# Two-layer hybrid trunk: SGU constants in another buffer, a planner that reckons a longer landing, and the last tile's sums kept in PSUM

## The chip, the cores and the metric

The kernel runs on one core of a Trainium2 chip. The metric is the device time of one execution in microseconds (us). Before the change the median of three runs is 1430.35 us (1429.0 to 1435.49).

## The reference, cut to what matters

Two layers run on a latent stream x of 512 tokens and a context of 256 tokens, both 1024 wide. Only the latent stream is returned, so the second layer (layer 1 below) keeps 512 rows at its end.

```
shift, scale, gate = split(silu(c) @ w_ada + b_ada, 3)
h = x * (1 + scale) + shift
a_q, ..., s_u, s_v, s_g, m_a, m_g, m_s = split(h @ w_in)
y_attn = attention(q, k_all, v_all) * silu(a_g)
y_gla  = gla_finish(o_forward + o_backward) * silu(g_g)
vn     = layer_norm(s_v, sgu_ln_g, sgu_ln_b)
mixed  = einsum('gts,bnsgc->bntgc', w_s, vn) + b_s
y_sgu  = s_u * mixed * silu(s_g)
m      = sigmoid(m_a) * (y_attn @ w_br_attn) + sigmoid(m_g) * (y_gla @ w_br_gla) + sigmoid(m_s) * (y_sgu @ w_br_sgu)
x_new  = layer_norm(ALPHA * x + gate * (m @ w_out), post_g, post_b)
```

All of it is float32. The kernel splits each float32 operand into a high and a low part and makes three matmuls of every product (high by high, high by low, low by high).

## The kernel before, in words

**A planner writes the order.** The program text does not run in its own order. Every operation goes through `_Eng` or `Sched.alt` into `Sched.record`, and `Sched.order` (from L225) then places all of them by a list simulation: each operation has a cost, dependencies, a priority and the buffers (tags, each with some slots) that it needs. `issue` repeats this 16 times with corrected priorities and emits the shortest plan. The result is one fixed order per engine (PE, DVE, ACT, POOL, and SP, which issues the DMAs). So a changed constant can move instructions anywhere. Two choices are the planner's as well: `tta` (an elementwise operation of two tensors) may go to DVE or POOL, `evac` to ACT or DVE. Since all is recorded through one place, nearly every instruction of the trace carries L421 (or L128 for those with two possible engines, L119 for grouped matmuls).

How the planner times a DMA is in these lines, L325 to L328: the transfer occupies the DMA engines for `cost`, and whoever waits for the data may start 700 ns later.

```
            if e == "SP":
                dma = max(dma, st + 1300.0) + cost
                free[e] = max(st + 60.0, dma - self.AHEAD)
                end = dma + 700.0
```

**The parts of a layer.** Projections of h with the columns of `w_in` (weights stream in as `raw` tiles of 256 KB and are split into `hi` on ACT and `lo` on DVE or POOL), attention, GLA, the SGU, then the branches `brA`, `brG`, `brS` (products of each branch with its weight, gated and summed into `mac`), and last the product with `w_out`, the residual sum and the layer norm. Projections that nothing needs soon are fill work: they are projected when PE would else have nothing to do (matmuls `p<-hlh,hi` and the like), parked in DRAM (the gates `m_a`, the SGU inputs), and loaded again later as `kept` or `sv`.

**The SGU of layer 1** (from L1224). `sv` (the parked s_v) is normalised per tile: bn_stats, bn_aggr, POOL's rsqrt, one `tensor_scalar`, then times `lg` and plus `lb`. `sgc` holds the constants `lg`, `lb`, `bs` and `wsT`, 256 KB each. Each normalised tile is multiplied with `wsT` on PE (matmuls `pt<-sgc,sv`); DVE adds `bs` and writes `ymix`, which is then multiplied with two loaded gates. `sgc` lies in tag "T3". Its only slot holds the attention output `yat` until `ysplit` has split it into `yh` and `yl`; after `sgc` the slot goes to `mac0`.

**The branches** (`branch`, in the same function). Branch A multiplies `yh`, `yl` with `w_br_attn`: matmuls `p<-yh,hi`, `p<-yl,hi`, `p<-yh,lo`, 12 to a group of output channels. The tag "p" has two PSUM slots. A slot is free when DVE has made `mac` from it, which needs the sigmoid of the parked gate: a DMA `kept<-md`, then ACT.

**The end** (`finish`, and the loop under `lab(f"{l}out")`). For each of the last four tiles of 128 rows, DVE adds the product in PSUM to the residual `r[t]` in SBUF in pieces of 256 columns and takes bn_stats. `finish` then computes mean and variance (bn_aggr), POOL the rsqrt in two small operations, DVE `nb = -mean * rstd`; DVE normalises the columns up to `cut` in two operations of three operands, ACT and POOL (one ACT, two POOL operations) the columns behind. `cut` is 832 (`LAST`) for the last tile and 608 (`CUT`) for the others. `r[t]` of the last tile is called rB, of the others rA.

Of the kernel before, what the change touches and what calls it, by code (L numbers as in the profile page):

```python
# [13 lines left out]
ALU = mybir.AluOpType  # L14
# [8 lines left out]
C_GQ, C_GK, C_GV, C_GG = 1280, 1536, 1792, 2336  # L23
C_SU, C_SV, C_SG = 2848, 3360, 3872
C_MA, C_MG, C_MS = 4384, 5408, 6432


class Sched:
# [109 lines left out]
    def order(self, prio):  # L138
# [31 lines left out]
        dma, cur, ticks, acted = 0.0, None, {}, 0.0  # L170
# [45 lines left out]
        while done < n:  # L216
            best = None
            for e in engs:
                L, R = later[e], ready[e]
                while L and (L[0][0] <= free[e] or gone[L[0][1]]):  # L220
                    a, i = heapq.heappop(L)
# [4 lines left out]
                t = free[e] if R else (L[0][0] if L else None)  # L226
# [7 lines left out]
            t, e = best  # L234
            R, L = ready[e], later[e]
            while L and L[0][0] <= t:
                a, i = heapq.heappop(L)
# [57 lines left out]
            st = t  # L295
            if e in held and e in self.port[i]:
                st = max(st, held[other[e]])
            if e == "ACT" and ops[i][5] not in (None, cur):
                st = max(st, acted + 1283.0)
                cur = ops[i][5]  # L300
            ks = set()
            for x in list(missing(i)):
# [11 lines left out]
                st = max(st, r_)  # L314
# [10 lines left out]
            if e == "SP":  # L325
                dma = max(dma, st + 1300.0) + cost
                free[e] = max(st + 60.0, dma - self.AHEAD)
                end = dma + 700.0  # L328
            else:
                end = free[e] = st + cost  # L330
                if e == "ACT":
                    acted = end
                if e in held and e in self.port[i]:
                    held[e] = end
# [17 lines left out]
            for j in succ[i]:  # L352
                g = ops[j][0]
                g = g[0] if isinstance(g, tuple) else g
                a = end + self.lag(e, g, i in ops[j][9])
# [149 lines left out]
def kernel(ctx: ExitStack, tc: tile.TileContext, A, out, dbg=None):  # L505
    nc = tc.nc
    sc = Sched(nc)
    ACT, DVE, POOL, PE, SP = sc.ACT, sc.DVE, sc.POOL, sc.PE, sc.SP
# [8 lines left out]
    def T(tag, shape, dt=F32, name=None):  # L517
        return sc.tile(sb, shape, dt, tag, BUFS.get(tag, 1), name or tag, "SB")

    def PS(tag, shape, dt=F32):  # L520
        return sc.tile(psp, shape, dt, tag, 2, tag, "PS")
# [11 lines left out]
    def act(out, in_, func=AF.Copy, **kw):  # L533
        return ACT.activation(out=out, in_=in_, func=func, **kw)

    def tt(eng, out, in0, in1, op):
        return eng.tensor_tensor(out=out, in0=in0, in1=in1, op=op)
# [6 lines left out]
    def stt(eng, out, in0, s, in1, op0, op1):  # L544
        return eng.scalar_tensor_tensor(out=out, in0=in0, scalar=s, in1=in1, op0=op0, op1=op1)
# [47 lines left out]
    AH, NPOOL, NP0 = 2, (0, 0), 0  # L593
    VB, SB, YB = 100, 0, 100
    DECAYS = [[(0, 0), (1, 0), (0, 1), (1, 1)]]
    CUT, LAST = 608, 832
    EARLY = (3, 3)
    FILL, GPROJ, EV = 8000.0, 4000.0, 20000.0
    WB = 20000.0
# [111 lines left out]
    def layer(l, X, start=None):  # L711
        full = l == 0
# [3 lines left out]
        q_t = all_t if full else lat_t  # L716
# [117 lines left out]
        for hf in range(2):  # L834
            wt = wgroup(w_in, 8, C_GV + 272 * hf, 272)
            for t in all_t:
                ps = tm(wt, 0, 272, X, t)
# [14 lines left out]
        for w, c0 in ((0, C_GK), (1, C_GQ)):  # L852
            wt = wgroup(w_in, 8, c0, 256)
            for pr in range(2):
                for seg in (["l", "c"] if (full or w == 0) else ["l"]):
                    ps = cm(wt, 128 * pr, 128, X, seg)
# [36 lines left out]
        for j in range(EARLY[l]):  # L893
            i, c4 = divmod(j, 4)
# [112 lines left out]
        for grp in DECAYS:  # L1007
            eg = {}
            for d, pr in grp:
# [4 lines left out]
                for c0, c1 in ((0, 512), (512, 768)):  # L1014
                    ps = PS("pt", [128, c1 - c0])
# [22 lines left out]
        for pr in range(2):  # L1038
# [31 lines left out]
            for d, seq in ((0, [0, 1, 2, 3, 4, 5]), (1, [1, 0, 5, 4, 3, 2])):  # L1070
                r = slice(64 * d, 64 * d + 64)
# [16 lines left out]
            for gi in range(2):  # L1088
# [4 lines left out]
                for lvs in LEVELS:  # L1093
                    ps = PS("s", [128, 2, 512])
                    calls, kq, views, off, cost = [], [], {}, 0, SWITCH_PE
                    for lv in lvs:
# [26 lines left out]
                        for ci in range(ng):  # L1123
                            for hh in range(2):
                                r = slice(64 * hh, 64 * hh + 64)
# [97 lines left out]

        lab(f"{l}sgu")  # L1224

        sgc = T("T3", [128, 4, 512], name="sgc")
        lg, lb, bs, wsT = (sgc[:, i] for i in range(4))
        SP.dma_start(out=lg, in_=A["sgu_ln_g"][l].partition_broadcast(128))
        SP.dma_start(out=lb, in_=A["sgu_ln_b"][l].partition_broadcast(128))
# [79 lines left out]
        r = {}  # L1309
# [87 lines left out]
        def finish(t):  # L1397
            st = T("sf", [128, 16])
            DVE.bn_aggr(out=st[:, 12:14], in_=stats[t])
            rsqrt_(st[:, 13:14], st[:, 13:14], 1, 1.0)  # L1400
            if full:
                ts(DVE, r[t], r[t], st[:, 12:13], ALU.subtract, st[:, 13:14], ALU.mult)
            if full:
                seg, off = ("c", t * 128) if t < 2 else ("l", (t - 2) * 128)
                si = 1 if t < 2 else 0
                for hf in range(2):
                    ps = PS("pt", [128, 4, 128])
                    for b in range(4):
                        k = 4 * hf + b
                        PE.transpose(ps[:, b], r[t][:, 128 * k:128 * k + 128], ident)  # L1410
                    h = T("Q2", [128, 4, 128], name="hx")
                    for b in range(4):
                        g_, b_ = (GB[:, si, w, 4 * hf + b:4 * hf + b + 1] for w in range(2))
                        sc.alt((ACT, "activation", dict(out=h[:, b], in_=ps[:, b], func=AF.Identity, scale=g_, bias=b_)),
                               (DVE, "tensor_scalar", dict(out=h[:, b], in0=ps[:, b], scalar1=g_, scalar2=b_, op0=ALU.mult, op1=ALU.add)))
                    split(Xn[seg][0][:, 4 * hf:4 * hf + 4, off:off + 128], Xn[seg][1][:, 4 * hf:4 * hf + 4, off:off + 128], h)
                if t >= 2:
                    SP.dma_start(out=x1d[(t - 2) * 128:(t - 1) * 128], in_=r[t])
            else:
                nb = st[:, 14:15]  # L1420
                stt(DVE, nb, st[:, 12:13], -1.0, st[:, 13:14], ALU.mult, ALU.mult)
                cut = LAST if t == q_t[-1] else CUT
                hs = slice(cut, 1024)
                act(r[t][:, hs], r[t][:, hs], AF.Identity, scale=st[:, 13:14], bias=nb)
                tt(POOL, r[t][:, hs], r[t][:, hs], pg[:, 0, hs], ALU.mult)
                tt(POOL, r[t][:, hs], r[t][:, hs], pg[:, 1, hs], ALU.add)
                SP.dma_start(out=out[(t - 2) * 128:(t - 1) * 128, hs], in_=r[t][:, hs])
                hs = slice(0, cut)
                stt(DVE, r[t][:, hs], r[t][:, hs], st[:, 12:13], pg[:, 0, hs], ALU.subtract, ALU.mult)
                stt(DVE, r[t][:, hs], r[t][:, hs], st[:, 13:14], pg[:, 1, hs], ALU.mult, ALU.add)  # L1430
                SP.dma_start(out=out[(t - 2) * 128:(t - 1) * 128, hs], in_=r[t][:, hs])

        lab(f"{l}out")
        wo = {}
        for c4, t in ([(c4, t) for c4 in range(4) for t in q_t] if full else
                      [(c4, t) for c4 in range(2) for t in q_t] + [(c4, t) for t in q_t for c4 in (2, 3)]):
            if c4 not in wo:
                wo[c4] = wgroup(A["w_out"][l], 8, 256 * c4, 256, ("T5", "T4") if c4 == 2 and not full else None,
                                None if full else gate[:, 0, 256 * c4:256 * c4 + 256])
            cs_ = slice(256 * c4, 256 * c4 + 256)  # L1440
            if True:
                ps = tm(wo[c4], 0, 256, Mx, t)
                if full:
                    tmp = T("F3", [128, 256], name="otmp")
                    tt(DVE, tmp, ps, gate[:, 1 if t < 2 else 0, cs_], ALU.mult)
                    stt(DVE, r[t][:, cs_], r[t][:, cs_], ALPHA, tmp, ALU.mult, ALU.add)
                else:
                    tt(DVE, r[t][:, cs_], ps, r[t][:, cs_], ALU.add)
                DVE.bn_stats(out=stats[t][:, c4], in_=r[t][:, cs_])
                if c4 == 3:  # L1450
                    finish(t)
        return Xn if full else None
# [184 lines left out]
```

## Time and profile before

| what | value |
|---|---|
| median of 3 runs | 1430.35 us (1429.0 to 1435.49) |
| the profiled execution's own time | 1431.16 us |
| its span | 1429.3 us |
| mean granted TensorE clock | 0.996 of full |
| PE busy | 1387.9 us (97%) |
| PE weight loads | 1227.5 us (86%) |
| DVE busy | 1032.5 us (72%) |
| ACT busy | 671.3 us (47%) |
| POOL busy | 164.5 us (12%) |

The span runs from the first to the last instruction of the profiled execution; what is left to its own time, 1.86 us, lies around it. Shares are means over stages with different limits: PE is the fullest engine over the whole, which does not tell which engine a given gap of PE waits for.

### The profile page before, as it was taken

How to read it: one execution, taken by the hardware profiler on the slowest of the kernel's cores; microseconds unless marked ns; L12 is line 12 of the kernel's file. 1: busy time of each engine (PE TensorE's matmuls, PEld its weight loads, DVE VectorE, ACT ScalarE, POOL GpSimd, SP SyncE). 2: the span in 40 equal slices, each digit the busy share in tenths (PEclk: the TensorE clock that was granted, in tenths of full speed). 3: DMA queues.
4: the chain of work that ended last, by engine and by line, in shares of the span. 5: the costliest groups of instructions: out<-in, count | busy, mean ns of one | idle time of the engine just before them, and what ended most of it. 6: DMA issues, size and time to landing. Idle time of an engine off the chain costs nothing.

```text
span 1429.3 us, 27382 instructions
## 1 busy us (share of the span) xinstructions
PE 1387.9 (97%) x10724; PEld 1227.5 (86%) x10724; DVE 1032.5 (72%) x2206; ACT 671.3 (47%) x1293; POOL 164.5 (12%) x261
## 2 busy tenths in 40 slices
PE   8999999999999999999999999999999998999997
PEld 5798899987888888888889999998987877888887
DVE  8968877897977678732147684897799876645396
ACT  4566667844464323212232174666774554422331
POOL 0021100034330000000000020110014320000003
PEclk9999999999999999999999999999999999999999
DMA  9410012332356765521224232112243467535542
GB/s 321 160 45 9 23 31 65 124 94 64 93 177 207 250 200 169 158 67 45 65 77 148 66 119 71 30 31 60 82 148 90 117 193 252 168 97 177 182 144 94
DMA packets 123956, 168.55 MB, mean 118 GB/s; under 512 B 9497, under 2 KB 90801, under 8 KB 123825
## 3 DMA queue, kind: packets, MB, share of 16 engines
q1 hardware_dynamic: 123826, 166.79, 37.4%
q8 instruction: 84, 1.38, 0.4%
q14 instruction: 46, 0.38, 0.1%
HBM read 143.41 MB, written 23.34 MB: 117 GB/s over the span
## 4 chain that ended last, share of the span: by engine, by line
PE 73%; DVE 16%; DMA 5%; issue 2%; ACT 2%; POOL 1%; SPq 0%; POOLq 0%; DVEq 0%; ACTq 0%
PE p L421 60%; PE pt L421 8%; PE s L421 4%; DVE M L128 3%; DVE lo L128 2%; DMA wada<-in_w_adaT_dram 2%; DVE wada L421 1%; DVE sm L421 1%; DVE junk L421 1%; DMA raw<-in_w_in_dram 1%; PE s L119 1%; DVE PTs L421 1%; DMA sgc<-in_sgu_b_dram 1%; DVE cs L421 1%; POOL sf L421 0%
## 5 line engine op out<-in xcount | busy, mean ns | idle before, releaser
L128 DVE TENSOR_TENSOR lo<-raw,hi 128x512 fp32r<-128x512 f32 (+1 forms) x293 | 202.4, 700 | 173.7 <-ACT hi L421 166.2
L421 ACT ACTIVATE hi<-raw 128x512 fp32r<-128x512 f32 (+1 forms) x296 | 185.8, 634 | 233.2 <-PE p L421 149.8
L421 PE MATMUL p<-hlh,hi 128*128 128x512 f32 x704 | 280.9, 399 | 2.5 <-DVE mac L421 1.5
L421 PE MATMUL p<-hlh,lo 128*128 128x512 f32 x704 | 280.7, 399 | 1.5 <-DVE lo L128 1.3
L421 PE MATMUL p<-hll,hi 128*128 128x512 f32 x704 | 278.6, 396 | 0.0
L421 PEld LDWEIGHTS p<-hlh,lo 128*128 128x128 f32 x704 | 132.4, 188 | 31.6 <-DVE lo L128 2.1
L421 PEld LDWEIGHTS p<-hlh,hi 128*128 128x128 f32 x704 | 132.3, 188 | 29.8 <-ACT hi L421 2.2
L421 PEld LDWEIGHTS p<-hll,hi 128*128 128x128 f32 x704 | 132.3, 188 | 26.5
L421 PE MATMUL p<-hch,lo 128*128 128x256 f32 x368 | 104.5, 284 | 0.0
L421 PE MATMUL p<-hch,hi 128*128 128x256 f32 x368 | 104.2, 283 | 0.0
L421 PE MATMUL p<-hcl,hi 128*128 128x256 f32 x368 | 104.0, 283 | 0.0
L421 PE MATMUL p<-hi,hlh 128*128 128x256 f32 (+1 forms) x352 | 102.0, 290 | 0.0
L421 PE MATMUL p<-hi,hll 128*128 128x256 f32 (+1 forms) x352 | 100.8, 286 | 0.0
L421 PE MATMUL p<-lo,hlh 128*128 128x256 f32 (+1 forms) x352 | 99.8, 284 | 0.0
L421 POOL TENSOR_SCALAR sf<-sf 128x1 f32<-128x1 f32 x20 | 7.5, 374 | 642.3 <-DVE sf L421 641.9
L421 PE MATMUL p<-yh,hi 128*128 128x512 f32 (+1 forms) x192 | 70.0, 364 | 7.8 <-DVE mac L421 6.7
L421 ACT ACTIVATE P<-s,sm 128x768 f32<-128x768 f32 (+1 forms) x80 | 65.4, 821 | 23.5 <-DVE sm L421 23.2
L421 DVE TENSOR_REDUCE sm<-s 128x1 f32<-128x768 f32 (+1 forms) x72 | 65.0, 921 | 12.4 <-PE s L421 12.2
L421 DVE TENSOR_TENSOR PTs<-pt,PTs 128x512 fp32r<-128x512 f32 x104 | 69.2, 685 | 4.1 <-ACT PTs L421 3.1
L421 PEld LDWEIGHTS p<-hcl,hi 128*128 128x128 f32 x368 | 69.3, 188 | 2.1
L421 PEld LDWEIGHTS p<-hch,hi 128*128 128x128 f32 x368 | 69.5, 189 | 1.9
L421 DVE SCALAR_TENSOR_TENSOR wada<-wada,srow 128x512 f32<-128x512 f32 x96 | 65.1, 687 | 8.0 <-DMA wada<-in_w_adaT_dram 6.7
(299 smaller groups left out, 3352.1 us busy)
## 6 DMA issues: line engine op xcount, KB each, us to landing
raw<-in_w_in_dram SPq DMA_DIRECT2D x204, 256.0 KB, 3.0
wada<-in_w_adaT_dram SPq DMA_DIRECT2D x80, 256.0 KB, 4.9
raw<-in_w_out_dram SPq DMA_DIRECT2D x32, 256.0 KB, 2.9
raw<-in_w_in_dram SPq DMA_DIRECT2D x16, 272.0 KB, 3.1
wada<-in_w_adaT_dram SPq DMA_DIRECT2D x8, 512.0 KB, 4.9
raw<-in_w_br_attn_dram SPq DMA_DIRECT2D x16, 256.0 KB, 3.4
raw<-in_w_br_gla_dram SPq DMA_DIRECT2D x16, 256.0 KB, 3.0
raw<-in_w_br_sgu_dram SPq DMA_DIRECT2D x16, 256.0 KB, 3.3
```

Source lines behind the costliest of these rows:

```text
L119: return self.record(eng.n, lambda: [getattr(eng.e, m)(*a, **k) for m, a, k in calls], outs, ins, cost, None, dens)
L128: fns[p.n] = lambda real=real, k=k: real(**k)
L421: return s.record(n, lambda: real(*a, **k), outs, ins, _cost(n, meth, outs, ins, k), _table(n, k), _dens(n, ins, k), _port(n, meth, outs, ...
```

## The change

It has five parts. The planner adds `LAND` = 2000 ns instead of 700 to a DMA's transfer time before its readers may start. `sgc` of layer 1 goes to tag "hc", which held the context's h (split into `hch` and `hcl`) and has two slots. The last tile's residual sums go to a PSUM tile `R` (tag "s", 1024 columns), from which the statistics are taken. Its `finish` makes `Z = (R - mean) * g` for all 1024 columns on DVE into a second PSUM tile of tag "s", while the rsqrt is still being made; then DVE makes `Z * rstd + b` for the first 848 columns, ACT `Z * rstd` for the other 176, and POOL adds b to these; `nb` is gone for this tile. `LAST` becomes 848, and the tile before the last is now cut there too, no longer at 608.

```diff
@@ class Sched, order
+LAND = 2000.0
...
                 dma = max(dma, st + 1300.0) + cost
                 free[e] = max(st + 60.0, dma - self.AHEAD)
-                end = dma + 700.0
+                end = dma + LAND
...
-    CUT, LAST = 608, 832
+    CUT, LAST = 608, 848
...
-        sgc = T("T3", [128, 4, 512], name="sgc")
+        sgc = T("T3" if full else "hc", [128, 4, 512], name="sgc")
...
+            elif t == q_t[-1]:
+
+                Z = PS("s", [128, 1024])
+                a, b = slice(0, LAST), slice(LAST, 1024)
+                stt(DVE, Z, R, st[:, 12:13], pg[:, 0], ALU.subtract, ALU.mult)
+                stt(DVE, r[t][:, a], Z[:, a], st[:, 13:14], pg[:, 1, a], ALU.mult, ALU.add)
+                SP.dma_start(out=out[(t - 2) * 128:(t - 1) * 128, a], in_=r[t][:, a])
+                act(r[t][:, b], Z[:, b], scale=st[:, 13:14])
+                tt(POOL, r[t][:, b], r[t][:, b], pg[:, 1, b], ALU.add)
+                SP.dma_start(out=out[(t - 2) * 128:(t - 1) * 128, b], in_=r[t][:, b])
             else:
...
-                cut = LAST if t == q_t[-1] else CUT
+                cut = LAST if t == q_t[-2] else CUT
...
+        R = None if full else PS("s", [128, 1024])
...
-                    tt(DVE, r[t][:, cs_], ps, r[t][:, cs_], ALU.add)
-                DVE.bn_stats(out=stats[t][:, c4], in_=r[t][:, cs_])
+                    o = R if t == q_t[-1] else r[t]
+                    tt(DVE, o[:, cs_], ps, r[t][:, cs_], ALU.add)
+                DVE.bn_stats(out=stats[t][:, c4], in_=r[t][:, cs_] if full else o[:, cs_])
```

`full` is true in layer 0 only. Because of the planner the order changes on all engines. Three places of it matter below.

**SP, the loads of `sgc` in layer 1.** Before, they stand behind a store of the parked gate `md_0`, and wait for DVE (the number behind a semaphore's name is not its value):

```order
436 L421 DMA md_0_1806<-keep 128x512 [waits DMAHW2_49,Activation_49]
437 L421 DMA sgc<-in_sgu_ln_g_dram 128x512 [waits DMAHW3_49,DVE_49]
438 L421 DMA sgc<-in_sgu_ln_b_dram 128x512 [waits DMAHW4_49]
439 L421 DMA sgc<-in_sgu_wT_dram 128x512 [waits DMAHW5_49]
440 L421 DMA sgc<-in_sgu_b_dram 128x512 [waits DMAHW6_49]
```

Now:

```order
346 L424 DMA sgc<-in_sgu_ln_b_dram 128x512
347 L424 DMA sgc<-in_sgu_wT_dram 128x512
348 L424 DMA raw<-in_w_in_dram 128x2x256 [waits DMAHW7_49,DVE_49]
349 L424 DMA sgc<-in_sgu_b_dram 128x512
350 L424 DMA pgx<-in_post_g_dram 128x1024 [waits PE_49]
```

The four loads (that of `lg` is the row ahead) have moved up by some 90 places, and the wait for DVE is gone.

**DVE, from the SGU of layer 1 to branch A.** Before, the `ymix` operations end shortly ahead of the first `mac`:

```order
1329 L421 TENSOR_TENSOR ymix<-pt,sgc 128x4x128 x3
1330 L128 TENSOR_TENSOR ymix<-ymix,kept 128x512 x4
1331 L128 TENSOR_TENSOR lo<-raw,hi 128x512
1332 L128 TENSOR_TENSOR ymix<-ymix,kept 128x512
1333 L128 TENSOR_TENSOR lo<-raw,hi 128x512
1334 L128 TENSOR_TENSOR ymix<-ymix,kept 128x512 x3
1335 L421 SCALAR_TENSOR_TENSOR wada,gs<-wada,srow 128x512
1336 L421 TENSOR_TENSOR mac_2215<-p,kept 128x512 x2
```

Now, from the last `ymix` on:

```order
1346 L131 TENSOR_TENSOR ymix<-ymix,kept 128x512
1347 L424 SCALAR_TENSOR_TENSOR wada,gs<-wada,srow 128x512 x2
1348 L131 TENSOR_TENSOR lo<-raw,hi 128x512 x3
1349 L424 SCALAR_TENSOR_TENSOR wada,gs<-wada,srow 128x512 x2
1350 L131 TENSOR_TENSOR lo<-raw,hi 128x512 x4
1351 L424 SCALAR_TENSOR_TENSOR wada,gs<-wada,srow 128x512 x2
1352 L131 TENSOR_TENSOR lo<-raw,hi 128x512
1353 L424 TENSOR_TENSOR mac_2215<-p,kept 128x512
```

The first `mac` now stands 14 instructions behind the last `ymix`, not one, and the loads and sigmoids of its gate stand further ahead on SP and ACT. On PE the last of the SGU's matmuls now stand 120 fill matmuls ahead of branch A's first; before, they stand among branch A's first twelve, and the fill is ahead of them. The order of PE shows it, before:

```order
6679 L421 MATMUL p<-yh,lo 128x512 [waits DVE_49]
6680 L421 MATMUL p<-yh,hi 128x512
6681 L421 MATMUL pt<-sgc,sv 128x128 [waits Activation_49]
6682 L421 MATMUL pt<-sgc,sv 128x128 x3
6683 L421 MATMUL p<-yl,hi 128x512
```

and now (behind the last of the SGU's matmuls the fill begins):

```order
6546 L424 MATMUL p<-hlh,lo 128x512
6547 L424 MATMUL pt<-sgc,sv 128x128 [waits DVE_49]
6548 L424 MATMUL pt<-sgc,sv 128x128 x3
6549 L424 MATMUL p<-hlh,hi 128x512 [waits Activation_49]
6550 L424 MATMUL p<-hll,hi 128x512
```

The fill ends at row 6668, and branch A's first matmul is row 6669:

```order
6667 L424 MATMUL p<-hll,hi 128x512
6668 L424 MATMUL p<-hlh,lo 128x512
6669 L424 MATMUL p<-yh,hi 128x512 [waits Activation_49]
6670 L424 MATMUL p<-yl,hi 128x512
6671 L424 MATMUL p<-yh,lo 128x512 [waits DVE_49]
```

So branch A now has 120 matmuls of other work ahead of it that need nothing of the SGU.

**The end, on DVE and ACT.** Before, DVE's last rows:

```order
1764 L421 BN_STATS st<-rB 128x6 [waits DVE_49]
1765 L421 BN_AGGR sf<-st 128x2 [waits DVE_49]
1766 L421 SCALAR_TENSOR_TENSOR rB<-rB,sf,pg 128x832 [waits DVE_49]
1767 L421 SCALAR_TENSOR_TENSOR sf<-sf 128x1 [waits Pool_49]
1768 L421 SCALAR_TENSOR_TENSOR rB<-rB,sf,pg 128x832 [waits DVE_49]
```

Now (`s` is the tag of R and Z):

```order
1765 L424 TENSOR_TENSOR s<-p,rB 128x256 [waits DVE_49,PE_49]
1766 L424 BN_STATS st<-s 128x6 [waits DVE_49]
1767 L424 BN_AGGR sf<-st 128x2 [waits DVE_49]
1768 L424 SCALAR_TENSOR_TENSOR s<-s,sf,pg 128x1024 [waits DVE_49]
1769 L424 SCALAR_TENSOR_TENSOR rB<-s,sf,pg 128x848 [waits DVE_49,Pool_49]
```

ACT's last instructions now:

```order
1113 L424 ACTIVATE hi<-raw 128x512 [waits DVE_49,PE_49,Activation_49] x2
1114 L424 ACTIVATE rA<-rA,sf 128x416 [waits DVE_49] x2
1115 L424 ACTIVATE rA<-rA,sf 128x176 [waits DVE_49]
1116 L424 ACTIVATE rB<-s,sf 128x176 [waits DVE_49]
1117 L1648 UNCONDITIONAL_BRANCH
```

The last ACT instruction reads the same PSUM tile as DVE's last, and the semaphore value that it waits for is the one that DVE reaches with that instruction.

## Rows read from the trace of the kernel before

**Rows 1.** The page, part 1: busy time, share of the span, instructions.

```profile
PE 1387.9 (97%) x10724; PEld 1227.5 (86%) x10724; DVE 1032.5 (72%) x2206; ACT 671.3 (47%) x1293; POOL 164.5 (12%) x261
```

**Rows 2.** Windows: start:end, length, busy PE, PEld, DVE, ACT, POOL, clock, DMA share, GB/s.

```profile
0.00:60.00 60.00, 50.93 (x231) 38.17 (x232) 53.49 (x174) 28.65 (x44) 0.77 (x8) 1.00 0.78 272
1000.00:1160.00 160.00, 157.75 (x1735) 133.04 (x1734) 141.40 (x332) 94.14 (x172) 41.19 (x78) 1.00 0.36 105
1160.00:1200.00 40.00, 39.16 (x187) 32.11 (x186) 24.07 (x39) 22.49 (x39) 1.20 (x2) 1.00 0.83 270
1205.00:1220.00 15.00, 9.79 (x34) 7.54 (x33) 10.13 (x22) 5.78 (x9) 0.00 (x0) 0.77 0.71 245
```

**Rows 3.** Timeline of PE at 1206 to 1217 us: start, duration, instruction, [idle before, releaser].

```profile
1206.33 0.39 PE L421 MATMUL p<-yh,lo 128*128 128x512 f32 x1
1211.93 0.80 PE L421 MATMUL p<-yh,hi 128*128 128x512 f32 x1 [5.21 <-DVE mac L421]
1212.52 0.63 PE L421 MATMUL p<-yl,hi 128*128 128x512 f32 x1
...
1216.71 0.40 PE L421 MATMUL p<-yh,lo 128*128 128x512 f32 x1
1216.94 0.40 PE L421 MATMUL p<-yh,hi 128*128 128x512 f32 x1
```

**Rows 4.** Timelines of DVE, ACT and SP's queue, 1176 to 1212 us.

```profile
1176.44 0.69 DVE L128 TENSOR_TENSOR yl<-yat,yh 128x512 fp32r<-128x512 f32 x1
1177.62 0.38 SPq L421 DMA_DIRECT2D sgc<-in_sgu_ln_g_dram  x1
1182.12 2.02 DVE L128 TENSOR_TENSOR sv<-sv,sgc 128x512 f32<-128x512 f32 x3 [2.25 <-DMA sgc<-in_sgu_ln_g_dram]
1203.05 0.69 DVE L421 TENSOR_TENSOR ymix<-pt,sgc 128x512 f32<-128x512 f32 x1 [0.20 <-PE pt L421]
1205.70 0.93 SPq L421 DMA_DIRECT2D kept<-md  x2
1209.23 1.28 ACT L421 ACT_TABLE_LOAD   x1 [2.02 <-DMA kept<-md]
1211.18 1.29 DVE L421 TENSOR_TENSOR mac<-p,kept 128x512 f32<-128x512 f32 x2 [0.69 <-ACT kept L421]
```

**Rows 5.** Waits of PE: total us, times, longest.

```profile
PE s L119 <- DVE M L128: 3.6, 5, 1.4
```

**Rows 6.** Timeline of the end, 1421 to 1429 us.

```profile
1421.17 0.42 DVE L421 TENSOR_TENSOR rB<-p,rB 128x256 f32<-128x256 f32 x1 [1.11 <-PE p L421]
1422.39 1.08 DVE L421 SCALAR_TENSOR_TENSOR rB<-rB,sf,pg 128x832 f32<-128x832 f32 x1
1422.44 1.08 POOL L421 TENSOR_SCALAR sf<-sf 128x1 f32<-128x1 f32 x1 [0.86 <-DVE sf L421]
1423.61 0.55 POOL L421 TENSOR_TENSOR sf<-sf,mhalf 128x1 f32<-128x1 f32 x1
1424.27 1.08 DVE L421 SCALAR_TENSOR_TENSOR rB<-rB,sf,pg 128x832 f32<-128x832 f32 x1
1424.39 0.55 ACT L421 ACTIVATE rB<-rB,sf 128x192 f32<-128x192 f32 x1 [5.11 <-DVE sf L421]
1425.01 1.45 POOL L421 TENSOR_TENSOR rB<-rB,pg 128x192 f32<-128x192 f32 x2 [0.85 <-ACT rB L421]
```

**Rows 7.** Timelines of DVE and POOL: the third tile's finish, a small POOL operation elsewhere.

```profile
1166.04 0.19 POOL L421 TENSOR_SCALAR sg<-sg 128x4 f32<-128x4 f32 x1 [6.59 <-DVE sg L421]
1416.77 0.85 DVE L421 SCALAR_TENSOR_TENSOR rA<-rA,sf,pg 128x608 f32<-128x608 f32 x1
1416.83 0.85 POOL L421 TENSOR_SCALAR sf<-sf 128x1 f32<-128x1 f32 x1 [0.83 <-DVE sf L421]
```

**Rows 8.** Groups of instructions by shape: busy, mean ns, idle before.

```profile
L421 ACT ACT_TABLE_LOAD x19 | 24.4, 1283 | 7.7 <-DMA kept<-md 5.0 <-DMA srow<-in_crow_dram 2.5
L128 DVE TENSOR_TENSOR M<-cs 128x192 f32<-128x192 f32 x54 | 21.2, 446 | 0.7 <-PE s L421 0.6
```

## The prediction

> **What bounds the kernel now.** I read the page's busy times first. PE is busy 97% of the span [rows 1]: 1429.3 - 1387.9 = 41.4 us of it are PE's idle time, and a change that leaves the matmuls as they are can win only from these and from stretches at a lower clock. The windows then show where they lie: some 9 us in the first 60 us, where DVE is busy 53.49 of 60 and the DMA engines 0.78; only 2.25 us in the whole stretch from 1000 to 1160 us, though DVE is there at 141.40 of 160; and 5.21 us in one piece between 1205 and 1220, where the granted clock is 0.77 on average [rows 2]. The timeline of PE shows that piece: the last matmul before it starts at 1206.33, the next at 1211.93, released by DVE's `mac`, and the matmuls behind it start some 0.42 us apart until 1216.71; then the spacing is 1216.94 - 1216.71 = 0.23 [rows 3]. [...] From 1206.33 to 1216.71 there are 12 intervals; at 0.23 they take 2.8 us, and they took 10.4. **The spot costs 7.6 us.** The end is the other place: 1429.3 less the last DVE add's start at 1421.17 [rows 6], about 8.1 us with no matmul.
>
> The timelines of DVE, ACT and SP tell why PE waits at 1206. The loads of `sgc` are issued at 1177.62, after the split of `yat` has given the slot free (1176.44 + 0.69); DVE waits 2.25 us for them at 1182.12, the last `ymix` out of PSUM is at 1203.05, and only then do the gates' slots come free: `kept<-md` is issued at 1205.70, ACT waits 2.02 us for it and loads a table (1.28), and `mac` begins at 1211.18 [rows 4]. All of the fill work is behind PE by then.
>
> **The change, part by part.**
>
> *sgc in "hc" and the longer landing (one term).* The order shows the four loads of `sgc` some 90 places further up, with no wait for DVE in front, and DVE's `sv` products among the GLA's. PE now has 120 fill matmuls between the SGU's last matmul and branch A's first. At 0.23 us [rows 3] they are 27.6 us, and the first two groups of branch A, 24 matmuls, another 5.5, before a `mac` is needed. In that time DVE has the rest of `ymix`, 14 instructions of wada and `lo`, and what lies ahead of them, all of 0.6 to 0.7 us; I count about 40, some 27 us. The margin is some 6 us, and the gate's load and sigmoid lie ahead of it. So I take the 7.6 us as gone: **-7.6**. Bounds: 0 (the gap turns up elsewhere) and -7.6; more than it costs cannot be won.
>
> *Work that moves to DVE and ACT.* The new order has 25 instructions fewer on POOL and 22 more on DVE, mostly the GLA's `M<-cs`, 0.446 us each on DVE for the larger form [rows 8]: 22 x 0.446 = 9.8 us. To the GLA of layer 1 come also the eight `sv<-sv,sgc` products, 2.02 for three [rows 4], so 5.4 us. Half of the first and all of the second give about 10 us more in the stretch from 1000 to 1160, where DVE has 160 - 141.4 = 18.6 us free [rows 2]. ACT gets four more table loads, 4 x 1.283 = 5.1 us [rows 8], where the decays are made. What PE pays for this lies between -2.25 us (its idle time in that stretch goes to nothing, since the data are there earlier) and +15 (all of 9.8 + 5.4 exposed). The nearest row is the one of now: at 88% DVE fill PE waits 3.6 us for `M` in the whole run, in five waits [rows 5], the rest is covered by fill matmuls. I take **+0.5**.
>
> *The other places where a load's landing counts.* With 2000 ns the planner orders loads earlier where it can. At the start the DMA engines are at 0.78 [rows 2], so an earlier issue cannot bring data much earlier: 0, bounds -1 and +1. Waits for DMA elsewhere are covered by fill work and cost nothing today but the ones above: 0.
>
> *The tile before the last, cut at 848.* Its two DVE operations grow by 240 columns each. By (1.08 - 0.85) / (832 - 608) = 1.03 ns a column [rows 6, 7] that is 2 x 0.25 us, and DVE waits 1.11 us for the last matmul afterwards [rows 6]: **0**. Were that cover gone, 0.5.
>
> *The last tile.* `Z` starts where the first operation of 832 columns does, 1422.39. By 1.03 ns a column, 1024 columns take 1.08 + 0.20 = 1.28, to 1423.67. POOL's rsqrt: beside the 832 columns its first operation took 1.08, beside 608 columns 0.85, each as long as the DVE operation beside it, but 0.19 where DVE left it alone [rows 6, 7]. So in these rows the two engines excluded each other while DVE read two tensors in SBUF. With R in PSUM, DVE reads one of them there. If POOL is then free, its 0.19 + 0.55 end at about 1423.2, ahead of `Z`; if it is not, they end at 1422.44 + 1.28 + 0.55 = 1424.27 and `Z`'s successor waits 0.6. I take free. [...] Then DVE makes 848 columns in 1.10, to 1424.81 instead of 1425.35. But ACT, which now starts at 1424.39 beside DVE [rows 6], must wait for that, since both read one PSUM tile: 176 columns, about 0.54, to 1425.39; POOL one addition, about 0.66 (two of 192 take 1.45), to 1426.12 with the 0.07 between them. Before it was 1425.01 + 1.45 = 1426.46: **-0.34**. Bounds: +0.3 (POOL not free) and -0.9 (ACT's share ended with DVE's).
>
> [...] The row of this kernel that reads PSUM, the add of 256 columns, took 0.42 [rows 6]; the line through 608 and 832 columns gives 0.49 for 256, so the sum keeps the line.
>
> **The sum** is made against the profiled execution: 1431.16 - 7.6 + 0.5 - 0.34 = 1423.7. The median of the runs shown, 1430.35, is 0.8 below that execution, so the median of the changed kernel should be **1422.9 us**. A difference under 0.5%, 7.15 us, can't be told from none here; "faster" begins at 1423.2, so the forecast stands just beyond that edge, and its own range, 1420 to 1426, lies on both sides.
>
> **The rivals.**
>
> *1. The gain goes into the GLA of layer 1.* PE's order is fixed; the SGU's last matmuls stand ahead of the 120 fill matmuls and wait for DVE. If DVE is behind there, PE waits, with its fill still in the queue behind. For: DVE is at 88% over the stretch and would go to about 95%. Against: PE waits so little there now. With half of the 15 us exposed: 1431.16 - 7.6 - 0.34 + 7.6 = 1430.8, as a median 1430: no change.
>
> *2. Slower: the same place, nearly all of it exposed.* The mechanism is DVE's lead over PE running out in the GLA of layer 1, so that each `M`, each `Ac` and each `sv` arrives late. All 15 us exposed, and one more stretch at the low clock as after 1206 (4.8 us at half speed, 2.3 lost): 1431.16 - 7.6 - 0.34 + 15 + 2.3 = 1440.5, as a median 1439.7. It decides the sign of a measurable change from 15.1 us of new waits on (7.6 + 0.34 + 7.15). For it speak the four table loads, which fall where ACT is needed for the decays; against it, that 18.6 us of DVE are free.
>
> *3. The gap stays at branch A.* The margin of 6 us is worked out from orders and durations of before; if DVE is 11 us late there, all 5 us of the gap are back, with the low clock behind: 1431.16 - 0.34 = 1430.8, as a median 1430.0.
>
> *4. The end wins nothing*, since POOL isn't free or PSUM costs more: the forecast with 0.0 to +0.3 in place of -0.34, so 1423.2 to 1423.5. It shifts the forecast over the edge and no more.
>
> **How the numbers follow.** The forecast has 0.60 (with rival 4 in 0.15 of it); of it 0.43 fall below 1423.2 and 0.17 above. Rivals 1 and 3 together have 0.29, all within 0.5%, rival 2 has 0.11 with 0.10 beyond it. Faster 0.43, same 0.47, slower 0.10. The range reaches from 1419 (small waits of the GLA gone, start 1 us better) to 1431.5, which takes in rivals 1 and 3; left out are rival 2 and a better case than any I can price. The forecast's own range of 1420 to 1426 holds about half.
>
> **What would show it.** Right: no wait of PE over 1.5 us between 1150 and 1250, the clock at 1.00 there, `sgc` landed well before the last `yl<-yat`; PE's waits for `M` at 2 to 6 us in total; POOL's small operation beside `Z` at about 0.2 us, ACT's last starting after DVE's last, and from the last add's start to the span's end 7.8 us in place of 8.1. Wrong: PE waits ahead of the SGU's matmuls or in the GLA that sum to over 4 us, or a gap ahead of the third group of branch A.

## The result, and the profile after

The changed kernel takes 1417.22 us (median of 4 runs, 1415.26 to 1418.64), against 1432.71 for the kernel before in the runs beside it: a ratio of 0.9893, 95% interval [0.9862, 0.9924]. I had forecast 1422.9 with a range of 1419.0 to 1431.5. The direction was right; the gain is about twice the forecast one, and the time lies below the range. In the later runs the kernel before had medians of 1429.2 to 1430.3, so the gain is 12 to 15.5 us.

The profiled execution has a span of 1414.5 us against 1429.3. The page, part 1, of the changed kernel (busy time, share, instructions), to be read beside [rows 1]:

```profile
PE 1386.5 (98%) x10724; PEld 1226.6 (87%) x10724; DVE 1039.7 (74%) x2228; ACT 678.5 (48%) x1298; POOL 149.3 (11%) x236
```

PE's work is the same, 1386.5 us; its idle time fell from 41.4 to 28.0 us. DVE has 22 instructions and 7.2 us more, POOL 25 instructions and 15 us fewer.

The windows of the changed kernel (start:end, length, busy PE, PEld, DVE, ACT, POOL, clock, DMA share, GB/s), for stretches that answer to [rows 2]; as the kernel is ahead by then, the GLA of layer 1 is taken 10 us earlier, where the window holds nearly the same number of matmuls (1737 against 1735):

```profile
0.00:60.00 60.00, 52.97 (x234) 39.44 (x235) 53.68 (x173) 29.33 (x45) 0.77 (x8) 1.00 0.77 272
990.00:1150.00 160.00, 159.52 (x1737) 133.88 (x1735) 145.80 (x345) 100.05 (x175) 36.56 (x71) 1.00 0.40 116
1150.00:1190.00 40.00, 39.73 (x227) 32.96 (x205) 26.23 (x47) 26.52 (x44) 1.50 (x2) 1.00 0.91 291
1190.00:1240.00 50.00, 50.00 (x217) 40.56 (x216) 31.05 (x62) 20.64 (x35) 0.00 (x0) 1.00 0.61 183
```

In the 50 us from 1190, where branch A of layer 1 is now, PE never stops, and the clock is 1.00: the stop of 5.21 us and the slow matmuls of [rows 3] are gone, where the granted clock was 0.51 on average from 1211.93 to 1216.71 us and 1.00 from 1216.80 to 1220. The timeline of PE at branch A of the changed kernel:

```profile
1163.78 1.05 PE L424 MATMUL pt<-sgc,sv 128*128 128x128 f32 x8
...
1193.04 0.39 PE L424 MATMUL p<-yh,hi 128*128 128x512 f32 x1
1193.27 0.39 PE L424 MATMUL p<-yl,hi 128*128 128x512 f32 x1
```

Between the SGU's last matmuls, at 1163.78, and branch A's first, at 1193.04, PE works through fill for 28 us.

That accounts for about half. PE's waits in the branches of layer 0 are the next part. The waits of PE (total us, times, longest) between 500 and 770 us in the kernel before:

```profile
PE p L421 <- DVE mac L421: 3.0, 3, 1.5
PE p L421 <- DVE sig L421: 1.0, 1, 1.0
```

and the same stretch, 497 to 762 us, in the changed kernel:

```profile
PE p L424 <- DVE mac L424: 0.5, 1, 0.5
```

Adding up PE's idle times of 0.15 us and more from its timeline, by stage, gives before and after: the start (to 60 us) 9.0 and 6.9; layer 0 up to its branches 8.3 and 6.9; branches of layer 0 4.0 and 0.5; from there to branch A of layer 1 5.5 and 4.0; branches of layer 1 5.2 and 0; the last product 0.2 and 0.9. The sum falls by 13.0 us. PE's busy time, in which the slow matmuls behind the stop count, falls by 1.4 more, and from the last matmul's end to the span's end it is 7.9 us instead of 8.2.

### The profile page after: what moved, and what is told of

Read it like the earlier page. It is cut to its first block, busy times and chain, and to the rows that moved or that the text cites. A ratio compares the mean times of both kernels' runs of the same rounds, so it can differ in the third digit from the quotient of the medians.

```text
span 1414.5 us, 27331 instructions
## 1 busy us (share of the span) xinstructions
PE 1386.5 (98%) x10724; PEld 1226.6 (87%) x10724; DVE 1039.7 (74%) x2228; ACT 678.5 (48%) x1298; POOL 149.3 (11%) x236
## 4 chain that ended last, share of the span: by engine, by line
PE 76%; DVE 14%; ACT 5%; issue 3%; POOL 1%; DMA 0%; POOLq 0%; SPq 0%; DVEq 0%; ACTq 0%
PE p L424 63%; PE pt L424 8%; PE s L424 4%; DVE M L131 2%; DVE lo L131 2%; ACT L424 1%; DVE junk L424 1%; PE s L122 1%; ACT ez L424 1%; DVE wada L424 1%; DVE sm L424 1%; DVE PTs L424 1%; DVE St L424 1%; ACT hi L424 1%; DVE qx L131 1%
## 5 line engine op out<-in xcount | busy, mean ns | idle before, releaser
L424 PEld LDWEIGHTS p<-hch,lo 128*128 128x128 f32 x368 | 69.2, 188 | 0.2
```

The costliest lines, as they stand in the source:

```text
L424: return s.record(n, lambda: real(*a, **k), outs, ins, _cost(n, meth, outs, ins, k), _table(n, k), _dens(n, ins, k), _port(n, meth, outs, ...
```

## The experiments

Each run changes the changed kernel or the kernel before, and each is timed against the kernel before on the same chip. "Fill" counts, in PE's order, the fill matmuls of layer 1 that stand between the GLA's last `s<-gv,Af` and the SGU's last matmul ("ahead"), and between that and branch A's first ("behind"); the projections of gates that are not parked, 432 such matmuls behind branch A's first, do not count. "Start" and "br. 0" are PE's idle us in the first 60 us and in the branches of layer 0, "long waits" those over 1.7 us around branch A of layer 1 (1160 to 1225 us) with their releaser.

| run | landing | sgc | end | fill ahead, behind | median us | ratio to before, 95% | start | br. 0 | long waits |
|---|---|---|---|---|---|---|---|---|---|
| before | 700 | T3 | old | 136, 0 | 1429 to 1433 | 1 | 9.0 | 4.0 | 5.2 mac |
| changed | 2000 | hc | new | 31, 120 | 1417.22 | 0.9893 [0.9862, 0.9924] | 6.9 | 0.5 | none |
| e1 | 700 | hc | new | 0, 0 | 1437.42 | 1.0045 [1.0029, 1.0062] | 9.4 | 2.6 | 3.6 o, 7.5 mac |
| e2 | 2000 | T3 | new | 169, 0 | 1425.05 | 0.9962 [0.9947, 0.9976] | 6.8 | 0.6 | 4.0 mac |
| e3 | 2000 | hc | old | 31, 120 | 1417.22 | 0.9908 [0.9891, 0.9925] | 7.7 | 0 | none |
| e4 | 2000 | T3 | old | 169, 0 | 1426.61 | 0.9973 [0.9963, 0.9983] | 7.4 | 0.4 | 4.3 mac |
| e5 | 700 | hc | old | 0, 0 | 1437.82 | 1.0061 [1.0048, 1.0073] | 9.7 | 0.9 | 3.6 o, 8.1 mac |
| e6 | 2000 in layer 1 | hc | new | 31, 120 | 1423.18 | 0.9956 [0.9943, 0.9970] | 8.8 | 2.1 | none |
| e7 | 3000 | hc | new | 123, 0 | 1427.63 | 0.9989 [0.9980, 0.9998] | 8.5 | 1.4 | 4.6 mac |
| e8 | 2000 | hc | new, cut 608 | 31, 120 | 1416.08 | 0.9910 [0.9895, 0.9925] | 7.6 | 0.6 | none |
| e9 | 700 | hc | new | 0, 120 forced | 1432.02 | 1.0009 [0.9994, 1.0023] | 9.5 | 2.7 | 4.1 o, 1.7 ACT |
| e10 | 3000 | hc | new | 4, 120 forced | 1425.97 | 0.9968 [0.9957, 0.9978] | 8.4 | 2.0 | 3.1 o |
| e11 | 2000 | hc | new | 151, 0 forced | 1422.66 | 0.9948 [0.9930, 0.9967] | 8.4 | 0 | 4.1 mac |
| e12 | 700 | T3 | old | 16, 120 forced | 1436.84 | 1.0045 [1.0029, 1.0060] | 8.7 | 4.4 | 10.2 sv |

### One part undone, or one alone (e1 to e5)

**e1**, the landing back:

```diff
-LAND = 2000.0
+LAND = 700.0
```

> The changed kernel with the landing set back from 2000 to 700 ns; sgc in hc and the new end stay. Theory S (the forecast's: moving sgc out of T3 closes the gap of 7.6 us ahead of branch A, the longer landing is worth nothing much): 7 to 8 us faster than before, some 1423 to 1425, with no gap over 1.5 us at branch A of layer 1, and the small waits of before (PE for mac in layer 0, 4 us) still there. Theory L (the longer landing is what brings the gates, weights and constants in time): the gap or a good part of it stays, and the time is within 3 us of before. Theory R (any new order of the planner falls out some us better or worse, by chance): no rule, anywhere between 1415 and 1433.

Measured: 1437.42 us, 0.45% slower than before. Theory S is out, and none of the three had a time so high. The timeline of PE in this run, from the GLA's end to branch A:

```profile
1194.53 0.39 PE L424 MATMUL s<-St,qx 128*128 128x128 f32 x2
1198.50 0.66 PE L424 MATMUL pt<-ident,o 128*128 128x128 f32 x4 [3.58 <-DVE o L424]
...
1211.79 0.39 PE L424 MATMUL p<-yh,lo 128*128 128x512 f32 x1
1219.66 0.80 PE L424 MATMUL p<-yh,hi 128*128 128x512 f32 x1 [7.48 <-DVE mac L424]
```

and its windows (columns as in [rows 2]):

```profile
1170.00:1180.00 10.00, 10.00 (x45) 8.10 (x44) 2.40 (x4) 2.98 (x5) 0.00 (x0) 1.00 0.46 136
1180.00:1190.00 10.00, 10.00 (x45) 8.11 (x44) 2.33 (x4) 2.98 (x5) 0.00 (x0) 1.00 0.48 158
1190.00:1200.00 10.00, 6.42 (x41) 5.65 (x40) 3.72 (x7) 5.06 (x8) 1.20 (x2) 0.97 0.71 223
1200.00:1210.00 10.00, 9.19 (x43) 7.68 (x42) 9.53 (x16) 7.29 (x13) 0.00 (x0) 0.68 0.97 328
1210.00:1220.00 10.00, 2.52 (x11) 1.78 (x10) 8.17 (x16) 5.78 (x9) 0.00 (x0) 0.83 0.87 284
```

From 1170 to 1190 PE does nothing but fill, and DVE and ACT are three tenths busy at most. Then the GLA's last output, the gates of yat, the SGU and the sigmoids all come at once: DVE at 9.5 of 10, the DMA engines at 0.97, and PE stands still with no fill left. All of the fill had been placed ahead of the GLA's last chunk.

**e2**, sgc back in T3:

```diff
-        sgc = T("T3" if full else "hc", [128, 4, 512], name="sgc")
+        sgc = T("T3", [128, 4, 512], name="sgc")
```

> The changed kernel with sgc of layer 1 back in T3; longer landing and new end stay. Theory S: the chain from the split of yat over sgc to the gates' slots is back, and with it 5 to 7.6 us: 1422 to 1425. Theory L: the planner now knows that sgc lands late and keeps fill work for PE there, so at most 2 us are lost: 1417 to 1419. Theory R: no rule.

Measured: 1425.05, 7.8 us more than the changed kernel, just over the 5 to 7.6 that theory S had for this part. Here too the fill stands ahead of the SGU's last matmul (169) with none behind, and PE waits for `mac`:

```profile
1205.43 0.80 PE L424 MATMUL p<-yh,hi 128*128 128x512 f32 x1 [3.96 <-DVE mac L424]
```

**e3**, the old end in the new order:

> The changed kernel with the old end (sums of the last tile in SBUF, cuts 832 and 608); longer landing and sgc in hc stay. All theories of the order: the part ahead of the end moves little. The end from the last DVE add's start to the end of the span goes from 7.56 back to 8.13 us, but DVE is then free when the last matmul ends (the new end made it wait 0.3 us), so the time rises by 0.2 to 0.4 us in all: 1417.5. Theory R: up to 3 us either way, since the planner's order changes ahead of it too.

Its edit takes back what the diff changes at the end (R, Z and the cuts). Measured: the median is that of the changed kernel, 1417.22. But PE's order and its last matmul (1406.59 against 1406.60 us) are the same, so the two profiles can be compared row by row, and there the old end takes longer: from the last matmul's end to the end of the span 9.0 us against 7.9. The cause is in the section on the hardware.

**e4**, the landing alone, in the kernel before:

```diff
-                end = dma + 700.0
+                end = dma + 2000.0
```

> The kernel before with the landing alone set to 2000 ns; sgc in T3, old end. Theory S: the start and the waits for mac of layer 0 get better, the gap at branch A stays: 1424 to 1427. Theory L: nearly all of the gain, 1418 to 1420, and PE's longest wait under 2 us. Theory R: no rule.

Measured: 1426.61, a gain of 3.7 us or 0.27%. The start and the branches of layer 0 got better (7.4 and 0.4), the wait for `mac` in layer 1 stayed at 4.3. That is theory S in kind, at the upper end of its time.

**e5**, sgc in hc alone, in the kernel before (the contrary edit to e2's):

> The kernel before with sgc of layer 1 in hc alone; landing 700, old end. The run with landing 700, sgc in hc and the new end was slower than before by 7 us, with PE waiting 3.6 us for the GLA's last o and 7.5 us for the first mac, and no fill work left behind either. Theory SL (sgc in hc is worth something only if the planner reckons with late data): this is slower than before as well, 1433 to 1439, with the same two waits. Theory S (sgc in hc closes the gap by itself, the new end spoilt the order in that run): 1422 to 1425. Theory R (chance of the planner): anything from 1420 to 1440.

Measured: 1437.82, with the same two stops as e1 (3.6 and 8.1 us). So the new end had no part in e1. Moving sgc is worth -7.8 us with the long landing (e2 to changed) and costs 8.6 us without it (e5 against the kernel before on its chip, 1429.21).

### Which landing, and where (e6, e7)

**e6**, long in layer 1 only (the label of an operation begins with its layer):

```diff
-                end = dma + LAND
+                end = dma + (LAND if str(ops[i][7]).startswith("1") else 700.0)
```

> The changed kernel with the landing at 2000 ns for the DMAs of layer 1 only, 700 in the start and layer 0. Theory SL: each stage has its own gain from the landing, so the start (2 us) and the mac waits of layer 0 (3.5 us) come back and layer 1 keeps its own: 1421 to 1424, no wait over 2 us at branch A of layer 1. Theory R: no rule, the gap may come back: up to 1432.

Measured: 1423.18, 6.0 us more than the changed kernel, no wait at branch A of layer 1. The start (8.8) and the branches of layer 0 (2.1) are as with 700. So the gain in layer 1 does not hang on the gain ahead of it.

**e7**, the landing at 3000:

> The changed kernel with the landing at 3000 ns. Theory SL: data are now reckoned even later; as the landings of the 256 KB loads that branch A waits for are 4 to 5 us from issue, most of the gain stays: 1415 to 1421, PE waits in the branches under 1.5 us. Theory R: the order is thrown again (DVE's order differs from that of the change in most places), and the time may be anywhere between 1415 and 1433.

Measured: 1427.63. Theory SL fails: the landing is reckoned longer still, but the order again has no fill behind the SGU, and the wait of 4.6 us for `mac` is back. What the nine orders so far share is the column "behind": wherever 120 stands there, there is no wait for `mac`; wherever 0 stands, there is one of 4.0 to 8.1 us.

### The place of the fill by itself (e9 to e12)

To test that cause directly, the planner got one more dependency, which no data need. In three runs the second group of the parked gates' matmuls (and so all later ones, since the slots of "p" are given out in the order of the text) may not be placed before the SGU's last matmul; in the fourth it is the other way round:

```diff
+            if not full and t == q_t[-1]:
+                sc.ops[mdg[1]][2].add(len(sc.ops) - 1)
```

where `mdg` lists the first matmul of each such group, and for e11

```diff
+                if not full and g == 0:
+                    sc.ops_dep = mdg[-1] + 23
                 PE.matmul(...)
+                if not full and g == 0:
+                    sc.ops[len(sc.ops) - 1][2].add(sc.ops_dep)
```

(the arguments of the matmul are left out here). This edit holds for each tile of 128 rows, so all four tiles' SGU matmuls stand behind the fill, and not only the last tile's, as the expectation has it.

**e11**, the changed kernel with the fill ahead:

> The changed kernel (landing 2000, sgc in hc, new end) with the contrary dependency: the matmuls of the SGU's last tile may not be placed ahead of the last of the parked gates' matmuls. The order then has no fill between them and branch A. Theory F: the gap is back, 4 to 6 us with 2 us of low clock: 1422 to 1426. Theory SL: the gates are reckoned late enough and no gap over 2 us comes: 1417 to 1419.

Measured: 1422.66, 5.4 us more than the changed kernel. The timeline of PE in this run:

```profile
1198.34 0.39 PE L424 MATMUL p<-yh,lo 128*128 128x512 f32 x1
1202.81 0.79 PE L424 MATMUL p<-yh,hi 128*128 128x512 f32 x1 [4.08 <-DVE mac L424]
1203.40 0.63 PE L424 MATMUL p<-yl,hi 128*128 128x512 f32 x1
```

With the same landing and the same buffers, putting the SGU behind the fill instead of ahead of it brings the gap back, with slow matmuls (0.63 us) behind it as in [rows 3]. That shows the cause of layer 1's gap.

**e9** and **e10**, fill behind with a landing of 700 and of 3000:

> The first run's kernel (sgc in hc, new end, landing 700: 7 us slower than before) with one dependency more in the planner alone: the second and all later groups of the parked gates' matmuls in layer 1 may not be placed ahead of the SGU's last matmul. The order then has 120 fill matmuls between that and branch A's first, as in the changed kernel, in place of none. Theory F (where the fill stands settles layer 1's gap; the landing only happened to lead the planner there): no wait over 2 us at branch A or for the GLA's last o, and 1421 to 1425, near the run with the long landing in layer 1 alone (1423). Theory SL (the long landing is itself what brings the gates in time): the wait for mac stays over 3 us, 1428 or more.

> The run with landing 3000 (1427.6, wait of 4.6 us for mac) with the same dependency. Theory F: the wait goes, with the low clock behind it, so 6 to 8 us less: 1419 to 1422. Theory SL: the landing was long already, so a dependency on fill changes nothing: 1426 to 1429.

Measured: 1432.02 and 1425.97, 7 and 4 us above what theory F had. It is half right. The wait for `mac` is gone in both (in e9 a wait of 1.7 us for ACT's `hi` is left at that place). But a new one stands at the GLA's last output; the timeline of PE in e9:

```profile
1169.57 0.39 PE L424 MATMUL s<-St,qx 128*128 128x128 f32 x2
1174.03 0.73 PE L424 MATMUL pt<-ident,o 128*128 128x128 f32 x4 [4.08 <-DVE o L424]
```

The GLA's last output needs ACT, DVE, POOL's rsqrt and DVE again before PE can transpose it, some 4 us, and here no fill stands in between (0 and 4 matmuls; the changed kernel has 31). Behind the GLA's last `s<-gv,Af` e9 and e10 have 120 and 124 fill matmuls in all, the changed kernel 151: the dependency kept 120 for the second stretch and left nearly none for the first. There are two serial stretches to cover, and the changed kernel's order covers both.

**e12**, fill behind in the kernel before, with sgc in T3:

> The kernel before (sgc in T3, landing 700, old end) with the dependency of the runs with fill behind. Here sgc can only be loaded after yat has been split, so PE must get something to do until then. Theory F with sgc needed: the gap at branch A goes, but PE waits ahead of the SGU's matmuls, which now have little fill in front of them, for 5 us or more: 1428 to 1440, no gain. If moving sgc is not needed at all: no such wait, and 1421 to 1424.

Measured: 1436.84, and PE waits where it was expected to; the timeline of PE:

```profile
1171.17 0.40 PE L421 MATMUL p<-hlh,lo 128*128 128x512 f32 x1
1181.73 2.50 PE L421 MATMUL pt<-sgc,sv 128*128 128x128 f32 x10 [10.16 <-DVE sv L128]
```

The wait for `mac` is gone, and 10.2 us of waiting for the normalised `sv`, which needs `sgc`, stand in its place. So with sgc in T3 there is a third stretch to cover, and the fill does not suffice for it. That is what moving sgc to hc does: it makes it possible to place the fill behind, and does not do so by itself (e1, e5).

### The cut of the tile before the last (e8)

```diff
-                cut = LAST if t == q_t[-2] else CUT
+                cut = CUT
```

> The changed kernel with the tile before the last cut at 608 as before; PE's order is the same to the last instruction. In the changed kernel DVE began the last add 0.34 us after the last matmul's end, being still at the 848 columns of the tile before; before the change it began 0.03 us after it. If that is a cost, DVE begins right away and the end is 0.3 us shorter, unless POOL, with two additions of 416 columns (1.09 each) still to do, makes the last rsqrt wait: then up to 1 us longer. I expect POOL to be late: 0 to +1 us, 1417 to 1418. The forecast's reckoning (no cost either way) expects no change.

Measured: 1416.08 against 1417.22, whose runs overlap: no difference that can be told. In the profile POOL is late as expected, so that DVE's last operation waits:

```profile
1408.78 2.20 POOL L424 TENSOR_TENSOR rA<-rA,pg 128x416 f32<-128x416 f32 x2 [1.04 <-ACT rA L424]
1410.03 1.29 DVE L424 SCALAR_TENSOR_TENSOR s<-s,sf,pg 128x1024 f32<-128x1024 f32 x1
1411.06 0.19 POOL L424 TENSOR_SCALAR sf<-sf 128x1 f32<-128x1 f32 x1
1411.92 1.10 DVE L424 SCALAR_TENSOR_TENSOR rB<-s,sf,pg 128x848 f32<-128x848 f32 x1 [0.59 <-POOL sf L424]
```

From the last matmul's end (1408.76) to the span's end it is 8.1 us against 7.9.

## Why the prediction was right and wrong, point by point

**sgc and the gap at branch A (-7.6): right in size and mechanism, incomplete in its cause.** PE's wait fell by 5.2 us and its busy time by 1.4, so 6.6 in all; undoing only the buffer costs 7.8 (e2). The 120 fill matmuls behind the SGU, on which the term rested, are what settles it (e11). But that the longer landing leads the planner to this order is luck as far as the runs show: at 3000 ns it does not (e7). And the text put the two edits into one term and so did not see that the buffer alone would make the kernel slower (e1, e5). Rival 3's margin held: the first `mac` waits for PE, not PE for it, as the timeline of DVE in the changed kernel shows:

```profile
1196.01 0.69 DVE L424 TENSOR_TENSOR mac<-p,kept 128x512 f32<-128x512 f32 x1 [0.77 <-PE p L424]
```

**"The other places where a load's landing counts: 0, bounds -1 and +1" was the step that failed.** By the table the six profiles with a landing of 700 ns in the start and layer 0 (before, e1, e5, e6, e9, e12) have a mean of 9.2 us of PE idle at the start and 2.8 in the branches of layer 0, the six with 2000 (changed, e2, e3, e4, e8, e11) 7.5 and 0.35. That is 4.2 us. The changed kernel without the long landing there (e6) takes 1423.18 us, where the forecast had 1422.9 for the whole change. That is 6.0 more by the medians; the profiles show 3.4 us of idle time, 1.8 of slow matmuls (from 335 to 345 us the granted clock is 0.83 on average, a spell that of the other five with 700 only e12 shares, where the matmuls of 512 columns from 339.0 to 342.4 us show 0.63 us in place of 0.39) and 0.3 at the end. A longer landing is not better as such: at 3000 (e7, e10) the two stages stand at 8.4 to 8.5 and 1.4 to 2.0.

The sign of it was in the trace of before, in the waits of PE for `mac`: 8.2 us in four waits, of which the one at 1211.93 is only 5.2. The other three are in layer 0. What `mac` itself stands behind there is a load of `wada`, a piece of the weight `w_ada` that DVE multiplies between the branch's operations. The timelines of SP's queue, DVE and PE in the kernel before:

```profile
507.95 1.24 SPq L421 DMA_DIRECT2D wada<-in_w_adaT_dram  x2
513.67 0.69 DVE L421 SCALAR_TENSOR_TENSOR prod<-wada,srow 128x512 f32<-128x512 f32 x1 [3.10 <-DMA wada<-in_w_adaT_dram]
515.02 0.69 DVE L421 TENSOR_TENSOR mac<-p,kept 128x512 f32<-128x512 f32 x1
515.76 0.50 PE L421 MATMUL p<-yh,hi 128*128 128x512 f32 x1 [1.50 <-DVE mac L421]
```

DVE works in a fixed order, so its wait of 3.10 us for the load delays the `mac` behind it, and PE waits 1.50 us for the slot of "p". Ahead of PE's other two waits DVE stands for such loads too, 2.11 us at 531.23 and 1.39 at 556.58. In the first 30 us of branch A of layer 0 DVE waits 6.5 us for such loads in the kernel before, 1.3 to 5.9 in the other five profiles with 700 there, 0 in all six with 2000, and 1.4 and 2.1 in the two with 3000.

In layer 1 the gates' loads came late [rows 4]; here they are not what `mac` waits for. They come in pairs, each for four `mac` operations; the last pair is issued at 509.29 and 510.76 in the kernel before, 3.7 and 5.2 us behind branch A's first matmul, and its sigmoids (515.35 and 517.01) are done long before the ninth `mac` at 528.05 needs them. In the changed kernel this pair comes later still, 12.4 us behind that matmul (515.26 against 502.88), and PE does not wait.

At the start the text argued that a busy DMA could not bring data earlier. But the order of the loads changed: the first tile of `w_in` is issued at 2.47 us instead of 3.43, and PE's first wait there, 2.54 us for the first split of h at 13.09 us, became 0.75 at 11.30. That the one comes from the other is argued, not shown.

**Work moved to DVE and ACT (+0.5): too high, and of the other sign.** In the GLA of layer 1 DVE has 145.80 us of work in 160, 4.4 more than in [rows 2], where the text reckoned with about 10. The eight `sv<-sv,sgc` products are in this window now (1088 to 1131 us); so other work of DVE has left it. PE's idle time in the GLA fell from 2.25 to 0.48. ACT's four more table loads (23 in place of 19, 1.28 us each) cost nothing that can be seen. Rivals 1 and 2 did not come about; that a slower kernel was near is shown by e1 and e5, by another way than rival 2's (the fill was spent too early). The 4.8 us at half speed in rival 2's sum are the stretch from 1211.93 to 1216.71 in the trace of before, with its granted clock of 0.51 and its matmuls 0.42 us apart in place of 0.23 [rows 3]; the changed kernel shows no such stretch at branch A.

**The end (-0.34): -0.32 from the last matmul's end, with two errors that nearly cancel.** The timeline of the end in the changed kernel answers to [rows 6]:

```profile
1405.93 1.09 DVE L424 SCALAR_TENSOR_TENSOR rA<-rA,sf,pg 128x848 f32<-128x848 f32 x1
1406.32 0.28 PE L424 MATMUL p<-hi,mll 128*128 128x256 f32 x1
1406.94 0.42 DVE L424 TENSOR_TENSOR s<-p,rB 128x256 f32<-128x256 f32 x1
1408.17 1.29 DVE L424 SCALAR_TENSOR_TENSOR s<-s,sf,pg 128x1024 f32<-128x1024 f32 x1
1408.22 0.19 POOL L424 TENSOR_SCALAR sf<-sf 128x1 f32<-128x1 f32 x1
1409.56 1.10 DVE L424 SCALAR_TENSOR_TENSOR rB<-s,sf,pg 128x848 f32<-128x848 f32 x1
1410.70 0.41 ACT L424 ACTIVATE rB<-s,sf 128x176 f32<-128x176 f32 x1 [4.12 <-DVE rB L424]
1411.18 0.55 POOL L424 TENSOR_TENSOR rB<-rB,pg 128x176 f32<-128x176 f32 x1 [2.14 <-ACT rB L424]
```

POOL's operation takes 0.19 beside `Z`, `Z` 1.29 (1.28 reckoned), 848 columns 1.10, and ACT starts behind DVE, all as forecast. That POOL would be free beside `Z` was my choice of two values, which no row of before showed; the 0.19 shows it. ACT and POOL were quicker than reckoned (0.41 for 0.54, 0.55 for 0.66): from the last add's start to the end of the span (1414.46 and 1429.33 to the hundredth) 7.52 us against 8.16, a gain of 0.64. But "the tile before the last, cut at 848: 0" failed by 0.31: DVE is still at that tile when the last matmul ends at 1406.60 and begins the add 0.34 later, where in the kernel before it was 0.03 (1421.14 to 1421.17).

That `Z` and its successor read PSUM does not show in their times: 1.29 and 1.10 us, against 1.28 and 1.10 on the line through the SBUF operations of 608 and 832 columns [rows 6, 7].

**Open.** Why the planner places the fill behind at 2000 ns and not at 700 or 3000, and why DVE's `wada` operations stand clear of their loads at 2000 and not wholly at 3000, isn't explained; each landing changes DVE's order in most places, and no run told the one decision that matters. Between the start and branch A of layer 1, outside layer 0's branches, PE's idle time fell by 2.9 us more (8.3 to 6.9 and 5.5 to 4.0), which no run takes apart. The start varies by 1.6 us among profiles with the same landing (6.8 to 8.4), so its 1.7 us have that much doubt.

## What to carry to other kernels

Where the order is fixed ahead, independent work is a stock that covers serial stretches: count in the order how much of it stands ahead of and behind each stretch, and compare that with the stretch's length, before judging what an edit to a buffer or a cost will do. An edit that removes a dependency can make such a kernel slower if the order spends its stock early (e1, e5), and two edits can gain more together than apart (alone the landing gained 3.7 us and the buffer lost 8.6). And where an engine waits for another, look at what that one waited for just before, in every stage: behind PE's small waits for `mac` in layer 0 stood a load that only DVE waits for, and the small waits of two stages came to over 4 us.

## What the runs showed of the hardware that I had not expected

In [rows 6, 7] it is POOL's small operation that takes as long as the DVE operation beside it. In e3 (old end, sums in SBUF) it is the other way round, and costs DVE: its first operation of 832 columns begins while POOL is at its two additions for the tile before:

```profile
1406.61 2.20 POOL L424 TENSOR_TENSOR rA<-rA,pg 128x416 f32<-128x416 f32 x2 [1.04 <-ACT rA L424]
1407.84 1.85 DVE L424 SCALAR_TENSOR_TENSOR rB<-rB,sf,pg 128x832 f32<-128x832 f32 x1
1408.89 0.85 POOL L424 TENSOR_SCALAR sf<-sf 128x1 f32<-128x1 f32 x1
```

It takes 1.85 us in place of 1.08 [rows 6]: it ends 0.88 us after POOL's additions, so most of it was done behind them. In e8 (shown above) POOL's same two additions run beside `Z`, which reads one operand in PSUM and one in SBUF, and `Z` takes 1.29 us as without them. So in these two profiles POOL's additions lengthen the DVE operation with two inputs in SBUF, by 0.77 us, and not the one with an input in PSUM. These 0.77 us are also why the new end is worth more in the new order (7.9 against 9.0 us from the last matmul's end) than against the kernel before (8.2), where POOL's additions ended at 1421.58, 0.81 us ahead of DVE's operation; the medians of e3 and of the changed kernel, both 1417.22, do not show it, so it rests on one profile of each.
